# Two transformer stacks on one core: head-pair scores on two row groups, modulation loads and the bias lookup spread over more steps

## The chip, the cores and the metric

The kernel runs on one core of a Trainium2 chip. The metric is the device time in microseconds (us) of one execution. A core has five engines that work side by side, each in the order of its own queue: TensorE (PE, with its weight loads as PEld), VectorE (DVE), ScalarE (ACT), GpSimd (POOL) and SyncE (SP), which here only issues DMAs. TensorE reads weights and moving data from SBUF and writes PSUM, which has eight banks of 128 partitions by 512 fp32 numbers.

## The reference, cut to what matters

`x` has 512 tokens of 1024 features. It goes through a first stack of two layers (latent attention and an MLP, then dilated attention and an MLP) and a second one of two (a recurrent mixer and a gated FFN, a Fourier and convolution mixer and a gated FFN). Every layer is modulated by vectors that are computed from the condition `c`:

```python
cond = silu(c)
mod = (cond @ ada_w[i] + ada_b[i]).reshape(B, N_MOD, D)      # 6 vectors of 1024 for a layer
h = rms_norm(x, norm_mix[i]) * (1 + scale1) + shift1
x = x + gate1 * mixer(h)
h = rms_norm(x, norm_mlp[i]) * (1 + scale2) + shift2
x = x + gate2 * (jnp.square(jax.nn.relu(h @ mlp_w1[i])) @ mlp_w2[i])
```

The dilated mixer has 16 heads of 64 features and three groups (window, dilation) of (128, 1), (512, 4) and (2048, 16). Each group gives scores with a bias that is looked up in a small table, an own softmax, and an output; the three are joined by their softmax denominators:

```python
bias = jnp.moveaxis(bias_table[bucket], -1, 2)
s = jnp.einsum('nbqhd,nbkhd->nbhqk', qb, kb) * (DIL_HEAD_DIM ** -0.5) + bias
lse = jax.nn.logsumexp(jnp.where(valid, s, -jnp.inf), axis=-1)
p = jnp.exp(s - lse[..., None])
o = jnp.einsum('nbhqk,nbkhd->nbqhd', p, vb)
wts = softmax(stack(lses), axis=0)
o = jnp.einsum('gbsh,gbshd->bshd', wts, stack(outs)) @ w_o
```

## The kernel before

`x` is kept transposed, as 8 tiles of 128 features by 512 tokens. All products are fp32 split into a high and a low fp32r part, so that one product is three matmuls (`mm3`: high by high at L423, L427, L428). The stages follow one another: latent attention to about 384 us of the trace, the first MLP (384 to about 810), dilated attention (to about 1495), the second MLP, the recurrent mixer, an FFN (2430 to 2830), the Fourier and convolution mixer, the last FFN.

Weights stream in chunks of 512 KB (`load_w`): SP issues the load into `wst` (two buffers), ACT writes the high part `whi` (L400), DVE the low part `wlo` (L401), three buffers each. One chunk feeds 24 matmuls of 512 columns.

All side work is written as generators, called fibers, in three queues (POST, WORK, LOW). After every six matmuls of a dense product `step()` is called and lets each queue advance by one piece; where a fiber says `yield w` it stands still for w steps. The order on each engine is then made by the framework's scheduler at build time, and each engine keeps it.

Three fibers matter here.

- `ada` computes one modulation vector in two halves. A half loads eight tiles of 256 KB (`adaw`, two buffers, issued by SP at L497, placed behind the latest weight load by `behind`), multiplies each by its condition value and adds it to `adacc` (DVE at L512 and L535, or POOL with two instructions at L532 and L533), splits the sum (`adah` on ACT at L517, `adal` at L518), and then two matmuls of 512 columns (L521, L522) sum over the partitions into the PSUM bank `aux`. The lines that set its steps are

```python
for k in range(KD + 1):
    ...
    yield self.pace
...
yield 4
ps = self.aux.tile([128, T], F32, tag="aux", name="aux")
nc.tensor.matmul(ps, lhsT=self.onesr, rhs=hi, start=True, stop=False)
```

  `pace` is set to 1 before the first MLP and to 2 behind it. In the first MLP, the vectors m105, m111 and m110 are in LOW. The MLP has four parts of 64 steps, 32 for `w1` and 32 for `w2`.
- `dil_bias` looks up the biases in the first MLP: 32 units, 80 chunks, each with two matmuls (L1070) of a one-hot tile `oh` (DVE L1044, made from `ib`, which ACT's queue loads) by the table, an eviction `ev` (L1074 DVE or L1078 ACT) and a store to the DRAM tensors B0 and B12. It yields once for a chunk.
- `attend(pr, x)` is the attention of a pair of heads e=0, 1, whose 64 features each lie in partitions 0 to 63 and 64 to 127 of the same q and k tiles. It runs in WORK beside the next pair's 40 dense steps (`dil_w_in`), for the last pair (7) beside the output product `dil_w_o`, of which the first 768 rows need the pairs 0 to 5 (`os0` to `os5`) and the other 256 the pairs 6 and 7 (`os6`, `os7`). For each head, for w=0 (the dense window) and w=1 (the two dilated groups), SP loads the bias tile `P` (512 KB); then come two sets i=0, 2. A set is one PSUM tile `S` (tag `s`, one buffer): for w=0 six matmuls of 64 rows by 256 columns (two blocks by three of `mm3`), for w=1 four fp32 matmuls of 64 rows by 128 columns (L1199; each is two entries of the trace). DVE adds the bias and takes the maximum (L1210), POOL negates it (L1212), ACT takes exp (L1214). A permutation of the statistics follows on PE (L1222, L1244), POOL scales `P` (L1254), PE turns it (L1267 to L1281) and multiplies by v (L1291 to L1300). PSUM holds `aux` (1 bank), the dense `mm` (2), `s` (1), `t` (2) and `o` (1).

## Time and profile before

| | |
|---|---|
| median of three runs | 3406.11 us (3398.97 to 3411.0) |
| the profiled execution | 3404.87 us |
| its span in the trace | 3403.1 us, so 1.8 us lie outside it |
| PE busy | 3223.0 us, 95% of the span |
| DVE, ACT, POOL busy | 1924.8, 1482.5, 938.7 us |
| TensorE clock granted, mean | 0.976 of full speed |

Busy time is what an engine spends on its instructions; on PE a matmul counts as busy for as long as it runs, at whatever clock. "PEclk" is the granted clock as a share of the full one. Times within a stage are read from windows of the trace; the stages' bounds above come from the same windows.

### The profile page before, as it was taken

To read this page: it belongs to the slowest core of one execution; us is meant where nothing else is said; L and a number is where in the kernel's file an instruction comes from. 1 tells how busy PE (TensorE), PEld (TensorE's weight loads), DVE (VectorE), ACT (ScalarE), POOL (GpSimd) and SP (SyncE) were. 2 spreads that over 40 slices of the span, in tenths; PEclk is the share of its full clock that TensorE was granted. 3 is DMA by queue.
4 is the path that set the end of the run, shared out by engine and by line. 5 is a ranking of instruction groups with operands and counts; after the bars stand their busy time and mean duration, and the time that the engine had idled before them with its cause. 6 is when DMAs were issued, how large, how long until landed. Compare 5 with 4: busy or idle time off the path is not lost.

```text
span 3403.1 us, 46679 instructions
## 1 busy us (share of the span) xinstructions
PE 3223.0 (95%) x17382; PEld 2522.1 (74%) x17382; DVE 1924.8 (57%) x3416; ACT 1482.5 (44%) x2720; POOL 938.7 (28%) x1005
## 2 busy tenths in 40 slices
PE   5898998998999999989999999899899999989998
PEld 4665876887777777768888777667678887778887
DVE  8777655435545434564354577745665556874343
ACT  3565433334555555544242454533342335553232
POOL 5454003002652222103422030350223524540000
PEclk8999999999999999989999999889999999999999
DMA  6433577524344322224544223432144444132222
GB/s 213 129 113 91 168 213 236 168 93 130 118 138 150 128 87 87 78 98 150 156 151 131 69 83 113 105 98 58 66 140 159 162 149 136 56 115 101 95 93 81
DMA packets 234709, 417.40 MB, mean 123 GB/s; under 512 B 66161, under 2 KB 115569, under 8 KB 234481
## 3 DMA queue, kind: packets, MB, share of 16 engines
q1 hardware_dynamic: 217280, 383.82, 35.8%
q10 hardware_dynamic: 17200, 30.58, 3.2%
q8 instruction: 137, 2.24, 0.3%
q14 instruction: 92, 0.75, 0.1%
HBM read 378.64 MB, written 35.69 MB: 122 GB/s over the span
## 4 chain that ended last, share of the span: by engine, by line
PE 76%; DMA 7%; DVE 6%; POOL 4%; ACT 3%; issue 2%; SPq 1%; ACTq 0%; DVEq 0%; POOLq 0%
PE mm L423 20%; PE mm L427 20%; PE mm L428 20%; DMA adaw<-in_ada_w 6%; PE s L1977 1%; POOL adacc L533 1%; DVE nt L676 1%; PE o L2045 1%; DVE h_lo L682 1%; DVE wlo L401 1%; PE s L1199 1%; PE o L954 1%; POOL adaw L532 1%; PE t L938 1%; PE t L2018 1%
## 5 line engine op out<-in xcount | busy, mean ns | idle before, releaser
L427 PE MATMUL mm<-h_lo,whi 128*128 128x512 f32 (+1 forms) x2280 | 889.1, 392 | 17.6 <-DVE h_lo L682 17.6
L423 PE MATMUL mm<-h_hi,whi 128*128 128x512 f32 (+1 forms) x2280 | 875.0, 393 | 18.3 <-ACT whi L400 6.7
L401 DVE TENSOR_TENSOR wlo<-wst,whi 128x1024 fp32r<-128x1024 f32 (+2 forms) x454 | 560.8, 1236 | 577.1 <-ACT whi L400 568.5
L428 PE MATMUL mm<-h_hi,wlo 128*128 128x512 f32 (+1 forms) x2280 | 884.5, 391 | 0.1
L400 ACT ACTIVATE whi<-wst 128x1024 fp32r<-128x1024 f32 (+2 forms) x454 | 455.5, 1005 | 639.1 <-PE mm L427 550.8
L427 PEld LDWEIGHTS mm<-h_lo,whi 128*128 128x128 f32 x2280 | 433.1, 190 | 118.4 <-DVE h_lo L682 24.3
L423 PEld LDWEIGHTS mm<-h_hi,whi 128*128 128x128 f32 x2280 | 427.5, 190 | 120.4 <-ACT h_hi L681 7.9
L428 PEld LDWEIGHTS mm<-h_hi,wlo 128*128 128x128 f32 x2280 | 432.8, 190 | 95.4 <-issue 1.5
L512 POOL TENSOR_SCALAR adacc<-adaw,cond_c 128x512 f32<-128x512 f32 x22 | 20.9, 948 | 788.6 <-DMA adaw<-in_ada_w 537.7
L533 POOL TENSOR_TENSOR adacc<-adacc,adaw 128x512 f32<-128x512 f32 x154 | 216.2, 1404 | 11.7
L427 PE MATMUL mm<-r_lo,whi 128*128 128x512 f32 (+1 forms) x560 | 211.3, 377 | 2.3 <-DVE r_lo L714 2.3
L428 PE MATMUL mm<-r_hi,wlo 128*128 128x512 f32 (+1 forms) x560 | 211.0, 377 | 0.0
L423 PE MATMUL mm<-r_hi,whi 128*128 128x512 f32 (+1 forms) x560 | 210.5, 377 | 0.0
L532 POOL TENSOR_SCALAR adaw<-adaw,cond_c 128x512 f32<-128x512 f32 x154 | 142.7, 927 | 202.2 <-DMA adaw<-in_ada_w 201.1
L535 DVE SCALAR_TENSOR_TENSOR adacc<-adaw,cond_c,adacc 128x512 f32<-128x512 f32 x154 | 121.7, 790 | 90.5 <-DMA adaw<-in_ada_w 89.4
L690 DVE SCALAR_TENSOR_TENSOR x<-mm,m,x 128x512 f32<-128x512 f32 (+1 forms) x130 | 85.4, 690 | 99.0 <-PE mm L428 98.8
L427 PEld LDWEIGHTS mm<-r_lo,whi 128*128 128x128 f32 x560 | 105.5, 188 | 23.8 <-DVE r_lo L714 3.1
L428 PEld LDWEIGHTS mm<-r_hi,wlo 128*128 128x128 f32 x560 | 105.6, 189 | 20.9
L423 PEld LDWEIGHTS mm<-r_hi,whi 128*128 128x128 f32 x560 | 105.6, 189 | 20.9
L1139 POOL TENSOR_TENSOR sq<-raw 128x512 f32<-128x512 f32 x48 | 58.2, 1213 | 156.8 <-ACT raw L1168 37.1
L1214 ACT ACTIVATE P<-P,neg 128x256 f32<-128x256 f32 (+1 forms) x128 | 62.2, 487 | 87.7 <-POOL neg L1212 87.6
L1346 DVE SCALAR_TENSOR_TENSOR u<-mm,vec,u 128x511 f32<-128x511 f32 x44 | 33.0, 749 | 115.9 <-ACT u L1345 115.8
(863 smaller groups left out, 5909.6 us busy)
## 6 DMA issues: line engine op xcount, KB each, us to landing
adaw<-in_ada_w SPq DMA_DIRECT2D x384, 256.0 KB, 3.0
wst<-in_mlp_w SPq DMA_DIRECT2D x128, 512.0 KB, 3.6
wst<-in_ffn_up SPq DMA_DIRECT2D x88, 512.0 KB, 3.6
wst<-in_dil_w_in SPq DMA_DIRECT2D x64, 512.0 KB, 3.5
P<-B SPq DMA_DIRECT2D x32, 512.0 KB, 4.7
wst<-in_ffn_down SPq DMA_DIRECT2D x32, 512.0 KB, 3.4
ib<-ix ACTq DMA_DIRECT2D x64, 129.0 KB, 4.9
B<-msk SPq DMA_DIRECT2D x16, 512.0 KB, 4.7
```

The costliest lines, as they stand in the source:

```text
L400: i = self.nc.scalar.activation(hi, st, AF.Copy)
L401: self.wlo = self.nc.vector.tensor_tensor(lo, st, hi.bitcast(F32), op=ALU.subtract)
L423: i = mm(out, lhsT=l[0], rhs=r[0], start=start, stop=False)
L427: mm(out, lhsT=l[0], rhs=r[1], start=False, stop=False)
L428: mm(out, lhsT=l[1], rhs=r[0], start=False, stop=stop)
L532: eng.tensor_scalar(tmp, a, w, 1.0, op0=ALU.mult, op1=ALU.mult)
L533: eng.tensor_tensor(acc, acc, tmp, op=ALU.add)
L535: eng.scalar_tensor_tensor(acc, a, w, acc, op0=ALU.mult, op1=ALU.add)
L676: nc.vector.scalar_tensor_tensor(t, half_of(self.x[k], h), g[k], r[h], op0=ALU.mult, op1=ALU.mult)
L690: i = self.nc.vector.scalar_tensor_tensor(x, ps, gate[m], x, op0=ALU.mult, op1=ALU.add)
L1139: nc.gpsimd.tensor_tensor(sq, raw, raw, op=ALU.mult)
L1214: nc.scalar.activation(t, t, AF.Exp, bias=neg[:, b:b + 1], accum_out=total[:, b:b + 1])
```

## The change

There are four edits. In `ada` the wait between the split and the two matmuls is six steps and not four. `pace` becomes 2 in `mlp`, as soon as the first `w1` product of a part has been written, instead of behind the whole first MLP: m105, which is then past its loads, is not touched, but m111 and m110 go at one load in two steps. `dil_bias` yields two steps a chunk. And `attend` is turned: the loop over w is outermost, then i; the score matmuls of both heads of a set are issued alternately, head 0 on partitions 0 to 63 and head 1 on 64 to 127, into two `S` tiles. For that `s` has two buffers, so that all eight banks are taken. There is a `yield` between matmuls and softmax, so that the count of steps stays 8. The two bias tiles of a w are loaded together.

```diff
@@ ada
             eng.tensor_tensor(lo, a, hi.bitcast(F32), op=ALU.subtract)
-            yield 4
+            yield 6
             ps = self.aux.tile([128, T], F32, tag="aux", name="aux")
@@ mlp
                 self.dense(f"mlp_w1_{l}", D, n, h, sink, psum, first=half_of if part == 0 else None)
+                self.pace = 2
                 self.dense(f"mlp_w2_{l}", n, D, r, self.residual(gate, end), psum, last=half_of if end else None)
@@ dil_bias
                     ib = load(*units[i + 2])
-                yield
+                yield 2
             done = (gi, q0, ev)
@@ dilated
-            sp = E(tc.tile_pool(name="dil_s", bufs=1, space=PSUM))
+            sp = E(tc.tile_pool(name="dil_s", bufs=2, space=PSUM))
@@ attend
-                for e in range(2):
-                    hd = pr * 2 + e
-                    o = slice(e * 64, e * 64 + 64)
-                    for w in range(2):
+                rows = [slice(e * 64, e * 64 + 64) for e in range(2)]
+                for w in range(2):
+                    mx, total = {}, {}
+                    for e in range(2):
+                        hd = pr * 2 + e
                         p = P[e, w] = work.tile([128, 4, 256], F32, tag="P", name="P", bufs=5)
...
+                    for i in (0, 2):
+
+                        S = [sp.tile([128, 2, 256], F32, tag="s", name="s") for e in range(2)]
+                        units = [[], []]
+                        for j in range(2):
+                            b = i + j
+                            if w:
+                                for g in range(2):
+                                    for e, o in enumerate(rows):
+                                        mm(S[e][:, j, g * 128:g * 128 + 128], lhsT=res(x[f"q{1 + g}"][o], b),
                                            rhs=res(x[f"k{1 + g}"][o], b), start=True, stop=True)
...
+                            else:
+                                k0 = min(max(128 * b - 64, 0), 256)
+                                for n, (a, c) in enumerate(((0, 0), (0, 1), (1, 0))):
+                                    for e, o in enumerate(rows):
+                                        mm(S[e][:, j], lhsT=res(x["q0"][a][o], b), rhs=x["k0"][c][o][:, k0:k0 + 256],
+                                           start=n == 0, stop=n == 2)
...
+                        yield
+                        for e in range(2):
...
+                        yield
@@ build
             n.mlp(0, g, sh, "m105", MLP_PARTS[0], 5)
-            n.pace = 2
```

**Modulation loads in the first MLP.** On SP's queue before, around the second half of m110 (`adaw` are its loads, `wst` the weight chunks; a weight load waits there for a free `wst` buffer):

```order
L497 DMA adaw_5018<-in_ada_w 128x512
L497 DMA adaw_5037<-in_ada_w 128x512
L390 DMA wst_5362<-in_mlp_w2_0 128x1024
L497 DMA adaw_5079<-in_ada_w 128x512
L497 DMA adaw_5098<-in_ada_w 128x512
L390 DMA wst_5408<-in_mlp_w2_0 128x1024
L497 DMA adaw_5116<-in_ada_w 128x512
L390 DMA wst_5440<-in_mlp_w2_0 128x1024
```

The eighth load of the half is adaw_5116. On PE before, the matmul that needs all eight (L521) stands among the matmuls of the chunk that was loaded as wst_5330, the one ahead of wst_5362:

```order
L423 MATMUL mm_5336<-h_hi5_3542,whi_5332 128x512
L427 MATMUL mm_5336<-h_lo5_3543,whi_5332 128x512
L521 MATMUL aux_5243<-adah_5157,onesr_82 128x512
L428 MATMUL mm_5336<-h_hi5_3542,wlo_5333 128x512
L423 MATMUL mm_5337<-h_hi5_3542,whi_5332 128x512
```

So the last load stands behind the second weight load after the chunk in which PE reaches L521, 16 of the 24 matmuls short of that chunk's end. On SP's queue after, the end of a half of m110 (its first one):

```order
L497 DMA adaw_4986<-in_ada_w 128x512
L390 DMA wst_5079<-in_mlp_w2_0 128x1024
L497 DMA adaw_5011<-in_ada_w 128x512
L497 DMA adaw_5037<-in_ada_w 128x512
L390 DMA wst_5128<-in_mlp_w2_0 128x1024
L390 DMA wst_5187<-in_mlp_w2_0 128x1024
```

and on PE after, the L521 of that half, behind the last matmul of the chunk wst_5079 (`whi_5081`):

```order
L427 MATMUL mm_5086<-r_lo7_5076,whi_5081 128x512
L428 MATMUL mm_5086<-r_hi7_5075,wlo_5082 128x512
L521 MATMUL aux_5175<-adah_5108,onesr_82 128x512
L522 MATMUL aux_5175<-adal_5109,onesr_82 128x512
L423 MATMUL mm_5193<-r_hi0_4704,whi_5130 128x512
```

Now the last load stands behind the weight load of the very chunk at whose end L521 stands. Counted in chunks, the place of L521 minus that of the last load (0 where L521 stands at the start of the chunk whose weight load is just ahead of that load) is -1.6, -1.9, -1.3 and -1.6 for the four halves of m111 and m110 before, and +0.8, +0.8, +1.0 and 0.0 after; ten halves in the second MLP, before, have -0.9 to +1.3.

**Scores.** On PE before, one set of w=0 of one head among the dense matmuls of the next pair:

```order
L423 MATMUL mm_7745<-h_hi0_6915,whi_7641 128x512
L423 MATMUL s_7654<-k0h_7196,q0h_7358 128x256
L427 MATMUL s_7654<-k0l_7197,q0h_7358 128x256
L428 MATMUL s_7654<-k0h_7196,q0l_7359 128x256
L427 MATMUL mm_7745<-h_lo0_6916,whi_7641 128x512
```

Of the six matmuls three are shown; the three of the next block read alike. After, two sets stand together, and the heads change at every matmul (s_8281 is head 0, s_8282 head 1):

```order
L428 MATMUL mm_8085<-h_hi7_6929,wlo_8081 128x512
L1210 MATMUL s_8281<-k0h_7813,q0h_8066 128x256
L1210 MATMUL s_8282<-k0h_7813,q0h_8066 128x256
L1210 MATMUL s_8281<-k0l_7814,q0h_8066 128x256
L1210 MATMUL s_8282<-k0l_7814,q0h_8066 128x256
L1210 MATMUL s_8281<-k0h_7813,q0l_8067 128x256
L1210 MATMUL s_8282<-k0h_7813,q0l_8067 128x256
```

Over all w=0 sets, 169 of the 176 possible changes of head are there. Of the w=1 sets, those of i=0 alternate as written; those of i=2 mostly stand like this, on PE after:

```order
L1202 MATMUL s_8413<-k1_7925,q1_8123 128x128
L1202 MATMUL s_8413<-k2_8013,q2_8170 128x128
L1202 MATMUL s_8413<-k1_7925,q1_8123 128x128
L1202 MATMUL s_8413<-k2_8013,q2_8170 128x128
L1202 MATMUL s_8414<-k1_7925,q1_8123 128x128
L1202 MATMUL s_8414<-k2_8013,q2_8170 128x128
```

Four matmuls of one head come ahead of four of the other (two of the latter are shown); 61 of 112 possible changes are there. All 64 sets of before stand in 40 groups now, 16 for w=0 and 24 for w=1.

**The last pair beside the output product.** On PE before, from the first permutation of pair 7 (L1222) on:

```order
L428 MATMUL mm_12725<-os6h_12711,wlo_12694 128x512
L1222 MATMUL s_12461<-w4_12459,dil_perm_7013 128x64
L423 MATMUL mm_12726<-os6h_12711,whi_12693 128x512
L427 MATMUL mm_12726<-os6l_12712,whi_12693 128x512
L428 MATMUL mm_12726<-os6h_12711,wlo_12694 128x512
L1244 MATMUL s_12494<-w4_12459,dil_perm_7013 128x32
L1267 MATMUL t_12538<-ident_84,P_12334 128x128 x4
L1267 MATMUL t_12545<-ident_84,P_12424 128x128 x2
```

Behind L1244 no dense matmul follows until `os7h` is there. After, from the second permutation on (L1254 there, the turns are L1277):

```order
L427 MATMUL mm_12562<-os4l_12300,whi_12557 128x512
L1254 MATMUL s_12526<-w4_12491,dil_perm_7013 128x32
L1277 MATMUL t_12570<-ident_84,P_12409 128x128
L428 MATMUL mm_12562<-os4h_12299,wlo_12558 128x512
L1277 MATMUL t_12570<-ident_84,P_12409 128x128
L423 MATMUL mm_12562<-os5h_12303,whi_12557 128x512
L1277 MATMUL t_12570<-ident_84,P_12409 128x128
L427 MATMUL mm_12562<-os5l_12304,whi_12557 128x512
```

Pair 7 now stands earlier in the output product: 46 dense matmuls lie between its second permutation and the first one that reads `os7h`, where there were none.

## Rows read from the trace of the kernel before

**Rows 1.** Page, part 1: busy us, share, instructions.

```profile
PE 3223.0 (95%) x17382; PEld 2522.1 (74%) x17382; DVE 1924.8 (57%) x3416; ACT 1482.5 (44%) x2720; POOL 938.7 (28%) x1005
```

**Rows 2.** Windows: stretch, us, busy PE PEld DVE ACT POOL, PEclk, DMA share, GB/s.

```profile
480.00:500.00 20.00, 15.16 (x62) 11.78 (x62) 11.83 (x23) 4.66 (x9) 0.00 (x0) 0.91 0.71 189
520.00:540.00 20.00, 15.85 (x64) 12.42 (x63) 7.92 (x16) 7.80 (x15) 6.01 (x7) 0.91 0.71 188
560.00:580.00 20.00, 15.20 (x59) 11.90 (x58) 12.72 (x22) 6.38 (x11) 6.83 (x6) 0.91 0.63 201
640.00:800.00 160.00, 160.00 (x694) 129.03 (x693) 58.43 (x63) 57.76 (x83) 1.08 (x1) 1.00 0.30 100
840.00:1454.00 614.00, 608.96 (x3095) 467.68 (x3093) 292.14 (x657) 335.76 (x685) 205.55 (x270) 1.00 0.35 113
```

**Rows 3.** PE's waits in the first MLP: us in total, times, longest.

```profile
PE aux L521 <- ACT adah L517: 13.8, 3, 4.8
PE look L1070 <- ACT ev L1078: 2.9, 3, 1.9
...
PE aux L521 <- ACT ssq L655: 1.7, 1, 1.7
```

**Rows 4.** Timeline of PE behind one such wait: start, us.

```profile
493.17 0.63 PE L427 MATMUL mm<-r_lo,whi 128*128 128x512 f32 x1
493.60 0.63 PE L428 MATMUL mm<-r_hi,wlo 128*128 128x512 f32 x1
```

**Rows 5.** DVE's waits in that stage, then POOL's timeline.

```profile
DVE adacc L535 <- DMA adaw<-in_ada_w: 25.3, 15, 4.1
...
525.60 0.70 POOL L532 TENSOR_SCALAR adaw<-adaw,cond_c 128x512 f32<-128x512 f32 x1 [5.32 <-DMA adaw<-in_ada_w]
```

**Rows 6.** Timeline of PE: a score set of w=0, one of w=1.

```profile
981.74 0.40 PE L423 MATMUL mm<-h_hi,whi 128*128 128x512 f32 x1
...
982.28 0.28 PE L427 MATMUL s<-k0l,q0h 64*128 64x256 f32 x1
982.40 0.28 PE L428 MATMUL s<-k0h,q0l 64*128 64x256 f32 x1
...
982.97 0.50 PE L427 MATMUL mm<-h_lo,whi 128*128 128x512 f32 x1
983.31 0.40 PE L428 MATMUL mm<-h_hi,wlo 128*128 128x512 f32 x1
...
967.39 1.16 PE L1199 MATMUL s<-k,q 64*128 64x128 f32 x8
968.48 0.50 PE L428 MATMUL mm<-h_hi,wlo 128*128 128x512 f32 x1
```

**Rows 7.** Timeline of PE in the recurrent mixer: halves of 64 rows alternating.

```profile
1928.42 0.49 PE L1830 MATMUL hU<-hv,kt 64*128 64x128 f32 x4
```

**Rows 8.** Windows (as rows 2) and PE's timeline at dilated attention's end.

```profile
1454.00:1476.00 22.00, 17.15 (x93) 10.19 (x92) 3.60 (x14) 6.72 (x15) 7.10 (x16) 0.76 0.08 25
1476.00:1484.00 8.00, 7.61 (x20) 5.57 (x21) 5.14 (x6) 3.30 (x5) 0.00 (x0) 0.58 0.37 123
...
1457.19 0.38 PE L1244 MATMUL s<-w,dil_perm 128*128 128x32 f32 x2 [1.84 <-DVE w L1240]
...
1475.22 0.73 PE L423 MATMUL mm<-os7h,whi 128*128 128x512 f32 x2 [1.36 <-ACT os7h L367]
```

**Rows 9.** Page, part 6 (bias tiles), then instructions of L1210 (ns min/median/max).

```profile
P<-B SPq DMA_DIRECT2D x32, 512.0 KB, 4.7
...
L1210 DVE CUSTOM_DVE_ANT_1 P<-s,P x64: 408/420/448, 890.8 to 1452.7; 128x256 f32<-128x256 f32 x64
```

**Rows 10.** Page, part 5, POOL; then PE's wait from 2830 us on.

```profile
L533 POOL TENSOR_TENSOR adacc<-adacc,adaw 128x512 f32<-128x512 f32 x154 | 216.2, 1404 | 11.7
...
L532 POOL TENSOR_SCALAR adaw<-adaw,cond_c 128x512 f32<-128x512 f32 x154 | 142.7, 927 | 202.2 <-DMA adaw<-in_ada_w 201.1
...
PE mm L423 <- ACT y4h L367: 7.2, 1, 7.2
```

More of the change, by code (lines that the diff above doesn't have):

```diff
@@ L1189, in attend @@
                             nc.sync.dma_start(out=p, in_=self.B0[:, hd].rearrange("b p j -> p b j"))
-                        mx, total = (st[:, 1, j, e] if w else nt[:, j, e] for j in range(2))
-                        neg = sm.tile([128, 4], F32, tag="neg", name="neg", bufs=4)
-                        for i in (0, 2):
-                            S = sp.tile([128, 2, 256], F32, tag="s", name="s")
-                            units = []
-                            for j in range(2):
-                                b = i + j
-                                if w:
-                                    for g in range(2):
-                                        mm(S[:, j, g * 128:g * 128 + 128], lhsT=res(x[f"q{1 + g}"][o], b),
-                                           rhs=res(x[f"k{1 + g}"][o], b), start=True, stop=True)
-                                    units.append((b, S[:, j].rearrange("p (g j) -> p g j", g=2), by_res[e][:, b]))
-                                else:
-                                    k0 = min(max(128 * b - 64, 0), 256)
-                                    self.mm3(S[:, j], [res(t[o], b) for t in x["q0"]], [t[o][:, k0:k0 + 256] for t in x["k0"]],
-                                             True, True)
-                                    c0, c1 = band(b)
-                                    s0 = 128 * b - 64 + c0 - k0
-                                    units.append((b, S[:, j, s0:s0 + c1 - c0], p[:, b, c0:c1]))
-                            for b, s, t in units:
-                                nc.vector.tensor_tensor_reduce(out=t, in0=s, in1=t, scale=1.0, scalar=-3e38,
-                                                               op0=ALU.add, op1=ALU.max, accum_out=mx[:, b:b + 1])
-                            nc.gpsimd.tensor_scalar(neg[:, i:i + 2], mx[:, i:i + 2], -1.0, 0.0, op0=ALU.mult, op1=ALU.add)
-                            for b, s, t in units:
-                                nc.scalar.activation(t, t, AF.Exp, bias=neg[:, b:b + 1], accum_out=total[:, b:b + 1])
-                            yield
@@ new lines, in attend @@
+                        mx[e], total[e] = (st[:, 1, j, e] if w else nt[:, j, e] for j in range(2))
+                    for i in (0, 2):
[7 more added lines that the diff above has]
+                                        mm(S[e][:, j, g * 128:g * 128 + 128], lhsT=res(x[f"q{1 + g}"][o], b),
+                                           rhs=res(x[f"k{1 + g}"][o], b), start=True, stop=True)
+                                for e in range(2):
+                                    units[e].append((b, S[e][:, j].rearrange("p (g j) -> p g j", g=2), by_res[e][:, b]))
+                            else:
[4 more added lines that the diff above has]
+                                           start=n == 0, stop=n == 2)
+                                c0, c1 = band(b)
+                                s0 = 128 * b - 64 + c0 - k0
+                                for e in range(2):
+                                    units[e].append((b, S[e][:, j, s0:s0 + c1 - c0], P[e, w][:, b, c0:c1]))
+                        yield
+                        for e in range(2):
+                            neg = sm.tile([128, 4], F32, tag="neg", name="neg", bufs=4)
+                            for b, s, t in units[e]:
+                                nc.vector.tensor_tensor_reduce(out=t, in0=s, in1=t, scale=1.0, scalar=-3e38,
+                                                               op0=ALU.add, op1=ALU.max, accum_out=mx[e][:, b:b + 1])
+                            nc.gpsimd.tensor_scalar(neg[:, i:i + 2], mx[e][:, i:i + 2], -1.0, 0.0, op0=ALU.mult, op1=ALU.add)
+                            for b, s, t in units[e]:
+                                nc.scalar.activation(t, t, AF.Exp, bias=neg[:, b:b + 1], accum_out=total[e][:, b:b + 1])
+                        yield
```

## The prediction

> **What bounds the kernel now.** I began with the page's busy times: PE is busy in 95% of the span and the next engine in 57% [rows 1], so time can only be won where PE idles, runs slower than it could, or does work that can be shortened. Windows of 20 to 600 us then show which stage has what. A stretch of pure dense work in the first MLP is full: 160.00 of 160 us busy with 694 matmuls at clock 1.00, which gives 160/694 = 0.2305 us for a dense matmul of 512 columns [rows 2]. So is nearly all of dilated attention, 608.96 of 614 us [rows 2]: what is cut from PE's work there comes off the time, as long as the other engines keep up; they are busy for a third to a half of it.
>
> Three stretches are not full or not short. First, the first MLP from 480 to 580 us, where three windows have 15.16, 15.85 and 15.20 busy us of 20 and a clock of 0.91 [rows 2]. PE's list of waits names the cause: the matmul of a modulation vector (L521) waits for the split of its sum three times, 13.8 us in all [rows 3]. Behind each wait matmuls start 0.43 us apart for a while (493.17, 493.60) [rows 4], nearly twice 0.2305: PE idled, and then ran at the lower of its two clock levels. What the sum waits for is the transfer: DVE stands 25.3 us in 15 waits for the tiles `adaw`, and POOL, which sums m110, waits 5.32 us for a tile whose last product PE needs 5 us later [rows 5]. Second, the score matmuls, which use only half of the array's rows. Third, the end of dilated attention: from 1454 to 1476 us PE is busy for 17.15 of 22 us at clock 0.76, and then for 7.61 of 8 us at 0.58 [rows 8].
>
> **A, modulation loads and lookups in the first MLP.** No instruction is added or removed; sixteen loads each of m111 and m110, their sums, the matmuls L521 and the lookups move to later steps. In the order before, L521 stands 1.3 to 1.9 chunks ahead of where its last load stands on SP's queue, after it stands 0.0 to 1.0 chunks behind. A chunk is 24 x 0.2305 = 5.5 us, so each half gets about two chunks, 11 us, and a wait was 4.8 us at most [rows 3]. The second MLP is the check: its ten halves have -0.9 to +1.3, and PE's waits there list none at L521. I take all three waits as gone: 13.8 us. The slow clock behind them goes too: 1.00 - 0.91 = 0.09 of 20 us is 1.8 us for each of three windows, 5.4 us [rows 2]. Of the waits for lookups, 2.9 us [rows 3], I count a third, since the one-hot tiles get more time but the chunks on PE are only some 12% further apart by the order. L521's wait for the norm's statistics, 1.7 us [rows 3], I leave in: in the order after, a vector's matmul stands at the norm again. The transfers that move go to a stretch with DMA share 0.30 instead of 0.71 [rows 2], where PE does not wait for weights. A = 13.8 + 5.4 + 1.0 = 20 us. Below, 7 us, if two of the three waits come back at their old length, 20 - 2 x (4.6 + 1.8); above, 26 us, if all lookup and norm waits go and some small ones beside them.
>
> **B, scores on two row groups.** Before there are 8 pairs x 2 heads x 2 sets = 32 sets of each kind. A w=0 set: from the dense matmul at 981.74 to the one at 983.31 there are 1.57 us, of which two dense matmuls (981.74 and 982.97) take 0.46, so the set costs 1.11 us [rows 6]. Its matmuls start 0.12 us apart (982.28, 982.40) [rows 6], six of them 0.72, so that 0.39 us is entering and leaving. A w=1 set takes 1.09 us from its first entry to the next dense matmul (967.39 to 968.48) [rows 6]; with the same 0.2 us of delay at the dense matmuls around it, it costs 1.29, of which eight slots of 0.112 are 0.90 and 0.39 again the edges. In all 32 x 1.11 + 32 x 1.29 = 77 us of PE.
>
> Does a pair on both halves overlap? No score matmul shows it, but L1830 does: four matmuls of 64 rows that alternate between the halves end 0.49 us after their start [rows 7], where four of L1199, all in one half, would take 1.16 - 4 x 0.112 = 0.71 (durations of rows 6 and 7). The difference, 0.22 us, is two slots for two pairs. So I count one slot saved for each change of head that the second matmul of a pair makes. For w=0, which alternates throughout, twelve matmuls take six slots: 16 groups x 6 x 0.12 = 11.5 us saved, and 16 edges of 0.39 fewer, 6.2 us. For w=1, 61 changes of head stand in the order after, since an entry's second pass follows in the same half and the sets of i=2 mostly go four and four: 61 x 0.112 = 6.8 us; 24 groups instead of 32 save 8 x 0.39 = 3.1 us. B = 11.5 + 6.2 + 6.8 + 3.1 = 28 us. Below: nothing overlaps and only the edges are saved, 9 us. Above: all w=1 sets overlap wholly, 112 instead of 61 slots and 8 more edges saved, 28 + 5.7 + 3.1 = 36 us.
>
> The Trainium skill's page "TensorEngine Tiling (Array Packing)", Overview, Theoretical Speedup, gives up to a factor of two where the contraction is 64 or less, and names no order in which the matmuls must stand. By it every slot of w=1 would be halved as well, which is the upper end just given; the one row that bears on it (L1830) alternates at every matmul, so no row shows what four and four do.
>
> What must keep up: the softmax of a set (L1210, two instructions of 0.42 us for a head, four for both) [rows 9] now comes at once for both heads, 1.7 us of DVE ahead of the low parts of the weights (L401) that are queued behind it. Those are one chunk, 5.5 us, ahead of PE, so I count nothing; without this cover it would cost up to 1.7 us for each of 32 groups, 54 us. The two loads of `P` are 512 KB each and land after 4.7 us (median) [rows 9]; that is the rival below.
>
> **C, the end of dilated attention.** Of the 22 us, 4.85 are idle; at 0.76 the 17.15 busy us lose 4.1; in the next 8 us, 0.4 idle and 0.42 x 7.61 = 3.2 are lost: 12.5 us [rows 8]. The reason is in the order: between pair 7's second permutation (1457.19) and the first matmul of `os7h` (1475.22) [rows 8] PE has only the turning and multiplying of pair 7, which wait for POOL's scaling and ACT's copies in turn. After, 46 dense matmuls, 10.6 us, stand in between, and the scores of that pair come earlier in the output product too. They cover the scaling, but not all: the last turns stand close to `os7h` again. C = 10 us; 0 if the dense matmuls wait for the same things in order, 12.5 if nothing is left.
>
> **D, losses elsewhere.** `pace` 2 holds from the first MLP on either way, but the two more steps a half stretch the vectors of the FFN: six vectors (m2012 and five behind it) now need 6 x 2 x (18 + 6) = 288 steps, before 264, and the FFN has 264. So a half of m2110 runs on into the next mixer: three of its products on POOL and the split stand there in the order after, ahead of the convolution's taps. A product is 0.93 + 1.40 us [rows 10]; with a split of 1.3 us, as POOL's L533 runs, three are 8.3 us. PE has one wait of 7.2 us there, at `y4h`, behind that convolution [rows 10], and it could grow by them all; POOL has room before its first tap, so I count 2 (0 to 8).
>
> Sum: 20 + 28 + 10 - 2 = 56 us. The profiled execution takes 3404.87 us, 1.8 of them outside its span and unchanged; 3404.87 - 56 = 3349 us. The median shown is 1.2 us above that execution, which is less than the runs differ.
>
> **Rivals.**
>
> *The row groups do not overlap* (the edit does not do what it says): B is 9 instead of 28, 3368 us. For it: PE takes its instructions in order, and each fp32 entry reloads its weights. Against: L1830 [rows 7].
>
> *Full overlap:* the four matmuls of one head start before the four of the other are through, since they share neither rows nor bank; B is 36, 3341 us. Against: in the rows a matmul starts behind the one ahead of it in the order [rows 6], and half the w=1 sets go four and four. The page named above would have this case.
>
> *The first MLP's waits stay:* the loads are spread, but they still stand behind weight loads that wait for their buffers, so the last of a half comes late; A is 7, 3362 us. For it: the last half has a lead of 0.0 chunks only. Against: the second MLP at the same leads.
>
> *The tail is not covered:* C is 0, 3359 us.
>
> *Slower:* a set's two `P` loads land one after the other, L1210 of the first head holds DVE in order, the low weight parts queue up behind it, and PE runs dry. There are 16 such pairs of loads; each that held PE for one landing, 4.7 us [rows 9], would cost 75 us in all, 3424 us. It decides from 56/16 = 3.5 us for each pair on. For it: DVE's order is fixed, and the second tile is wanted sooner after its issue than before. Against: L401 works a chunk, 5.5 us, ahead, so a hold must be longer than that before PE sees it, and the DMA share is 0.35 there [rows 2].
>
> **How the numbers follow.** Forecast 0.65, rivals in the order above 0.12, 0.06, 0.08, 0.05 and 0.04. The range: downward full overlap with A at 26 and D at 0 gives 3349 - 8 - 6 - 2 = 3333, with C at its end 3330, and I put 3328; upward the row groups' failure together with returned waits gives 3349 + 19 + 13 = 3381, and 3384 with some of D. The likeliest case alone has 3335 to 3368. Under 0.3%, 10 us, this kernel's measurement cannot tell a change. All cases but the last lie over 10 us below 3406; a mild form of the last would make it no change: faster 0.92, same 0.04, slower 0.04.
>
> **What would show it.** A right: no wait at L521 for `adah` in the first MLP, clock 1.00 in every window from 480 to 580. B right: a w=0 group of twelve within 1.2 us of PE, w=1 groups of i=0 shorter than those of i=2, and dilated attention from 840 to its tail shorter by some 25 to 30 us. C right: idle time and low clock around `os7h` down to 2 or 3 us. D: the wait at `y4h` longer than 7.2 us by 2. Wrong would be: twelve w=0 matmuls in 1.8 us, waits of PE for `wlo` in dilated attention with DVE at L1210 ahead of them, or new waits at L521 in the FFN or the second MLP.

## The result and the profile after

The changed kernel takes 3368.86 us, median of four runs (3362.55 to 3370.5), against 3404.61 us for the kernel before (four runs, 3398.97 to 3411.0): the ratio is 0.9891 (95% interval 0.9869 to 0.9913). That is 36 us where 56 were forecast; it lies in the range. Its profiled execution took 3370.5 us. The page of the profile after, its span and the line that answers to [rows 1]:

```profile
span 3368.7 us, 46642 instructions
...
PE 3191.8 (95%) x17382; PEld 2504.8 (74%) x17382; DVE 1923.2 (57%) x3416; ACT 1478.4 (44%) x2720; POOL 932.9 (28%) x1005
```

PE's share is unchanged at 95%, on a span that is 34.4 us shorter. Where they went is read by stage. Every stage begins with a norm whose first matmul sums the squares (L654), so the distance from one such start to the next in PE's timeline is the length of a stage:

| stage | before, us | after, us | difference | forecast |
|---|---|---|---|---|
| first MLP | 425.1 | 406.7 | -18.4 | A -20 |
| dilated attention with `dil_w_o` | 686.4 | 661.0 | -25.4 | B -28 and C -10 |
| second MLP | 370.0 | 372.0 | +2.0 | 0 |
| recurrent mixer | 582.0 | 582.7 | +0.7 | 0 |
| first gated FFN | 387.9 | 387.5 | -0.4 | 0 |
| Fourier and convolution mixer | 173.4 | 180.3 | +6.9 | D +2 |
| last FFN, to the last norm | 381.0 | 381.0 | 0.0 | 0 |

**First MLP.** Windows of that stage of the kernel after (columns as in [rows 2]):

```profile
480.00:500.00 20.00, 20.00 (x91) 15.99 (x91) 11.26 (x17) 4.99 (x9) 0.00 (x0) 1.00 0.83 235
520.00:540.00 20.00, 20.00 (x91) 16.03 (x90) 7.96 (x7) 8.25 (x15) 13.41 (x12) 1.00 0.71 203
540.00:560.00 20.00, 16.81 (x68) 13.21 (x68) 9.10 (x13) 8.38 (x15) 5.72 (x5) 0.91 0.57 163
560.00:580.00 20.00, 20.00 (x88) 16.13 (x87) 13.57 (x25) 3.24 (x4) 8.00 (x7) 1.00 1.01 314
640.00:790.00 150.00, 150.00 (x689) 122.80 (x688) 60.37 (x68) 51.34 (x71) 8.19 (x7) 1.00 0.32 115
```

Where 480, 520 and 560 read 0.91 before, they read 1.00 and are full. New holes have come at 540 us and, smaller, at 580 us (17.89 busy us of 20); from 640 us to the stage's end PE is full, as before. PE's waits in that stage of the kernel after name their cause:

```profile
PE look L1071 <- ACT ev L1079: 5.2, 4, 3.2
PE look L1071 <- DVE ev L1075: 2.1, 1, 2.1
```

None is at L521 any more (13.8 us in [rows 3]). The lookups wait instead, 7.3 us where they had 2.9.

**Scores.** PE's timeline of the kernel after: a w=0 group, a w=1 group of i=0, a w=1 group of i=2, each with the dense matmul behind it:

```profile
1173.72 0.39 PE L1210 MATMUL s<-k0h,q0h 64*128 64x256 f32 x2
1173.94 0.28 PE L1210 MATMUL s<-k0l,q0h 64*128 64x256 f32 x2
1174.06 0.28 PE L1210 MATMUL s<-k0h,q0l 64*128 64x256 f32 x2
...
1174.62 0.50 PE L423 MATMUL mm<-h_hi,whi 128*128 128x512 f32 x1
...
1180.15 1.16 PE L1202 MATMUL s<-k,q 64*128 64x128 f32 x16
1181.24 0.50 PE L423 MATMUL mm<-h_hi,whi 128*128 128x512 f32 x1
...
1185.64 1.71 PE L1202 MATMUL s<-k,q 64*128 64x128 f32 x16
1187.28 0.50 PE L423 MATMUL mm<-h_hi,whi 128*128 128x512 f32 x1
```

Two w=0 matmuls (x2) start in each slot, 0.12 us apart; the group of twelve takes 1174.62 - 1173.72 = 0.90 us, as long as six took before [rows 6]. The alternating w=1 group of sixteen entries takes 1181.24 - 1180.15 = 1.09 us, as eight took before. The one that goes four and four takes 1.64 us. The 40 groups of the order after are 23 of w=0 and 17 of w=1, in the trace and in the kernel's order alike, not 16 and 24; before, the 64 sets stood in 40 and 34 pieces, since dense matmuls cut some of them.

**What took half of that back.** Windows of dilated attention after:

```profile
840.00:900.00 60.00, 54.93 (x268) 42.98 (x267) 31.37 (x81) 32.52 (x71) 38.05 (x40) 0.96 0.41 136
900.00:960.00 60.00, 60.00 (x327) 45.49 (x326) 23.74 (x53) 28.48 (x56) 34.37 (x40) 0.95 0.41 131
960.00:1020.00 60.00, 55.38 (x278) 42.15 (x279) 31.45 (x65) 35.62 (x74) 25.18 (x32) 0.94 0.41 133
1020.00:1080.00 60.00, 56.05 (x299) 43.02 (x298) 31.45 (x71) 32.14 (x66) 20.81 (x28) 0.94 0.34 106
1140.00:1200.00 60.00, 60.00 (x328) 46.19 (x326) 31.90 (x79) 36.42 (x79) 14.10 (x20) 1.00 0.35 118
```

Before, the stretch from 840 to 1454 us has clock 1.00 and 5 us of idle time in 614 [rows 2]. After, its first 240 us have 13.6 us of idle time. The clock takes 0.04, 0.05, 0.06 and 0.06 of the busy time there, 11.9 us at most: the mean clock of a window also covers time in which PE stood still, and counted matmul by matmul (each start to the next, half of it where the clock stood at the lower level) it is 10.3 us. From 1140 us to the tail the stage is full again. PE's waits in those 240 us of the kernel after, and ACT's wait for the negation there, before (L1214) and after:

```profile
PE mm L423 <- ACT raw L1167: 7.2, 3, 4.6
PE t L1277 <- POOL P L1264: 5.0, 6, 1.2
...
ACT P L1214 <- POOL neg L1212: 32.9, 19, 5.1
ACT P L1224 <- POOL neg L1222: 34.4, 11, 7.9
```

`raw` is the eviction of a dense tile; PE waited 2.1 us for it there before. The turns of `P` (L1277) wait for POOL's scaling. In total ACT waits for the negation no longer than before, but in 11 pieces instead of 19, and in longer ones. The longest hole, followed through four engines of the kernel after (DVE, POOL, ACT, PE; in brackets the idle time and its releaser):

```profile
955.50 0.08 DVE L1220 DVE_READ_ACCUMULATOR2_ANT st<- 128x1 f32 x1
...
959.30 0.69 POOL L532 TENSOR_SCALAR adaw<-adaw,cond_c 128x512 f32<-128x512 f32 x1 [1.22 <-DMA adaw<-in_ada_w]
960.08 1.26 POOL L533 TENSOR_TENSOR adacc<-adacc,adaw 128x512 f32<-128x512 f32 x1
961.32 0.19 POOL L1222 TENSOR_SCALAR neg<-st 128x2 f32<-128x2 f32 x1
...
961.54 0.51 ACT L1224 ACTIVATE P<-P,neg 128x256 f32<-128x256 f32 x1 [7.90 <-POOL neg L1222]
...
963.52 1.05 ACT L1167 ACTIVATE raw<-mm 128x512 f32<-128x512 f32 x1
...
964.62 0.79 PE L423 MATMUL mm<-h_hi,whi 128*128 128x512 f32 x1 [4.62 <-ACT raw L1167]
965.21 0.63 PE L427 MATMUL mm<-h_lo,whi 128*128 128x512 f32 x1
965.64 0.63 PE L428 MATMUL mm<-h_hi,wlo 128*128 128x512 f32 x1
```

DVE has both maxima of the first head at 955.58. POOL waits for a modulation tile, multiplies and adds it, and only then, at 961.32, 5.7 us later, comes to the negation of these maxima, which takes 0.19 us. ACT has stood still for 7.90 us, does the exps of both heads, and at 963.52 reaches `raw`, which is queued behind them. PE needs that bank: 4.62 us idle, and then, with starts 0.6 and 0.43 us apart, the lower of its two clock levels, where it had run at 1.00.

**The end of dilated attention.** Windows around the first matmul of `os7h` after, and that matmul:

```profile
1418.00:1434.00 16.00, 14.61 (x104) 9.87 (x102) 4.25 (x6) 6.19 (x11) 0.00 (x0) 1.00 0.16 50
1434.00:1442.00 8.00, 6.13 (x24) 4.35 (x24) 7.88 (x10) 4.76 (x7) 0.00 (x0) 1.00 0.43 146
...
1432.04 0.73 PE L423 MATMUL mm<-os7h,whi 128*128 128x512 f32 x2 [1.36 <-ACT os7h L367]
```

The clock stays at 1.00, and the idle time is 1.4 and 1.9 us, where [rows 8] had 4.85 and 0.4 and the clock at 0.76 and 0.58. The wait at `os7h` itself is the same 1.36 us.

**The mixer behind the FFN.** POOL's timeline after, where the convolution's taps (L1402, L1392 before) begin:

```profile
2830.18 2.33 POOL L532 TENSOR_SCALAR adaw<-adaw,cond_c 128x512 f32<-128x512 f32 x2 [9.96 <-DMA adaw<-in_ada_w]
...
2833.73 1.29 POOL L1402 TENSOR_TENSOR cp<-cp,tap 128x512 f32<-128x512 f32 x1
2834.99 2.28 POOL L533 TENSOR_TENSOR adacc<-adacc,adaw 128x512 f32<-128x512 f32 x1
2837.22 1.29 POOL L1402 TENSOR_TENSOR cp<-cp,tap 128x512 f32<-128x512 f32 x1
```

POOL first waits 9.96 us for a modulation tile, so the first tap starts 40.2 us into the stage instead of 36.1. Two sums, a product and the split of m2110 then stand between the first five taps; a tap by itself costs 1.3 us. PE's wait at `y4h` is 7.2 us as in [rows 10]; the stage is 6.9 us longer because what leads up to it comes later.

### The profile page after: what moved, and what is told of

The parts are those of the page before. It is cut to its first block, busy times and chain, and to the rows that moved or that the text cites. A ratio compares the mean times of both kernels' runs of the same rounds, so it can differ in the third digit from the quotient of the medians.

```text
span 3368.7 us, 46642 instructions
## 1 busy us (share of the span) xinstructions
PE 3191.8 (95%) x17382; PEld 2504.8 (74%) x17382; DVE 1923.2 (57%) x3416; ACT 1478.4 (44%) x2720; POOL 932.9 (28%) x1005
## 4 chain that ended last, share of the span: by engine, by line
PE 78%; DVE 8%; DMA 4%; POOL 4%; ACT 3%; issue 2%; SPq 0%; ACTq 0%; DVEq 0%; POOLq 0%
PE mm L423 21%; PE mm L427 20%; PE mm L428 20%; DMA adaw<-in_ada_w 4%; DVE nt L676 1%; PE s L1987 1%; POOL adacc L533 1%; DVE h_lo L682 1%; POOL cp L1402 1%; POOL adaw L532 1%; PE o L2055 1%; DVE wlo L401 1%; PE look L1071 1%; PE t L2028 1%; PE o L955 1%
## 5 line engine op out<-in xcount | busy, mean ns | idle before, releaser
L517 ACT ACTIVATE adah<-adacc 128x512 fp32r<-128x512 f32 x44 | 27.7, 629 | 147.6 <-POOL adacc L533 105.3
```

## Experiments

Each kernel ran beside the kernel before, whose median was 3407.06 us with the first four, 3412.41 with the next four and 3409.5 with the last four. Times of single executions of one kernel differ by 5 to 15 us, so what an edit does is read from the stage in its trace as well; the stage lengths are those of the table's kind. They vary too: with dilated attention as in the kernel after, the six traces of after, e2, e4, e5, e8 and e12 have 657.3 to 661.0 us for it, and the eleven traces with the pacing of the kernel after in the first MLP, or with four steps in place of six, have 406.4 to 415.5 us there.

**One half of the change at a time.** `e1` has only the three pacing edits, `e2` only the attend with its two S buffers.

```diff
 # e1, against the kernel before
-            yield 4
+            yield 6
...
+                self.pace = 2
...
-                yield
+                yield 2
...
-            n.pace = 2
```

> Kernel before with the three pacing edits alone (six steps, pace 2 in the MLP, two steps a lookup chunk). If the parts add up as the trace after splits them (first MLP 18.7 us shorter, the start of the Fourier and convolution mixer 6.6 us longer): 3404.6 - 12 = 3392.5 us, no wait at L521 in the first MLP. Rival, the pacing edits are worth nothing by themselves or hurt dilated attention too: 3400 or more.

Measured: 3395.86 us, ratio 0.9969 (0.9959 to 0.9979). First MLP 406.5 us (-18.6), dilated attention 688.9, Fourier and convolution mixer 180.0 (+6.6). The parts of the trace hold.

```diff
 # e2, against the kernel after
-            yield 6
+            yield 4
...
-                self.pace = 2
...
-                yield 2
+                yield
...
+            n.pace = 2
```

> Kernel before with the turned attend and two S buffers alone. Theory (the new waits of the first head pairs come from the turned attend itself, whose negations and exps come in bursts): dilated attention 6 us shorter in its body and 17 in its tail, 3404.6 - 23 = 3381 us, clock below 1.00 in several windows of the first 240 us of dilated attention. Rival (those waits come from the modulation vectors that the six steps moved): the body gains the whole 30 us, 3357 us, clock 1.00 there.

Measured: 3383.27 us, ratio 0.9931 (0.9917 to 0.9944). Dilated attention 659.9 us (-26.4, 23 expected), the first MLP 425.8 and the mixer 172.5 as before. The product of the two ratios is 0.990, the change's is 0.9891: the halves add up. PE's waits at L521 for `adah` in the first MLP of e2 are there again, 11.9 us in three, and the windows of its dilated attention have losses of the same kind:

```profile
840.00:900.00 60.00, 57.91 (x273) 45.62 (x272) 28.40 (x59) 30.39 (x60) 26.57 (x27) 0.97 0.46 142
900.00:960.00 60.00, 56.30 (x292) 42.53 (x291) 29.49 (x55) 32.79 (x62) 36.65 (x44) 0.94 0.43 135
960.00:1020.00 60.00, 56.52 (x282) 44.51 (x281) 34.45 (x84) 34.33 (x75) 35.48 (x43) 0.94 0.45 143
1020.00:1080.00 60.00, 58.74 (x320) 45.16 (x319) 31.15 (x83) 33.45 (x72) 17.01 (x27) 1.00 0.40 121
```

That is 10.5 us of idle time, where the kernel before has 2.7. The single waits are others: 2.7 us for `raw`, 3.7 for DVE's `w`, 2.7 at L521 and L522. So new waits come with the turned attend, not with the loads that were moved, and which ones come depends on what else stands in the queues. The rival, 3357 us, is out.

**The negation on another engine.** `e3` moves the negation of the maxima from POOL to DVE.

```diff
-                            nc.gpsimd.tensor_scalar(neg[:, i:i + 2], mx[e][:, i:i + 2], -1.0, 0.0, op0=ALU.mult, op1=ALU.add)
+                            nc.vector.tensor_scalar(neg[:, i:i + 2], mx[e][:, i:i + 2], -1.0, 0.0, op0=ALU.mult, op1=ALU.add)
```

> Kernel after with the negation of the maxima on VectorE instead of GpSimd. Theory (a negation of 0.19 us stands on GpSimd behind the products of a modulation vector that wait for their loads; ACT's exps wait for it in order, the eviction of a dense tile behind them, and PE for that): ACT's wait for the negation falls from 34 us to under 10 between 840 and 1080 us, PE's waits for raw from 8.1 to under 4, clock 1.00 in most windows there; 12 to 17 us gained, 3354 us. Rival (the eight exps of two heads in one piece, 5 us of ACT, hold the eviction back whoever negates): 3366 to 3370 us, waits for raw as before.

Measured: 3370.99 us, ratio 0.9897 (0.9881 to 0.9912), no gain. ACT's waits of that kernel from 840 to 1080 us:

```profile
ACT P L1224 <- DVE neg L1222: 18.0, 7, 6.6
```

It fell from 34.4 to 18.0 us, not under 10. The hole near 960 us is gone, PE's waits for `raw` are 5.9 us (8.1 after), two windows have 0.97 and the rest 1.00, and dilated attention took 654.4 us in that execution. In `e10`, with the same negation, it took 658.3; the kernels with it on POOL have 657.3 to 661.0. The negation's place is thus worth a few us at most, not 12 to 17, and e10's 658.3 leaves open whether it is worth anything: the theory names the longest hole rightly and is not the whole cause. The rival's time, 3366 to 3370 us, is nearly met, its waits for `raw` are not.

**The modulation sums away from POOL.** `e9` leaves the negation on POOL and takes what it stood behind away.

```diff
-                                            nc.gpsimd if l and j % 2 == 0 else nc.vector))
+                                            nc.gpsimd if l and j == 0 else nc.vector))
```

> Kernel after with the sums of m112 and m114, the two modulation vectors that GpSimd computes beside the first head pairs, on VectorE. Theory (the products that wait for their loads hold the negation on GpSimd): ACT's wait for the negation between 840 and 1080 us falls from 34 to under 15 us, the wait of 4.6 us for raw near 960 us goes, dilated attention 6 to 10 us shorter than in the two traces of the kernel after (748.6 and 746.2 us from its first dense matmul to the output product's end). Rival (the exps of two heads hold the eviction, or VectorE's sums now hold the additions of the bias in the same way): 743 us or more, and raw waits of 7 us or more.

PE's wait for `raw` in dilated attention of that kernel:

```profile
PE mm L423 <- ACT raw L1167: 5.3, 4, 1.5
```

Dilated attention took 649.0 us in this one trace, 8 to 12 less than in those of the kernel after (6 to 10 were expected). From 840 to 1080 us PE is idle for 6.1 us, 13.6 after: it waits 3.9 us for `raw`, the longest 1.5, and 2.2 for the scaling of `P`. ACT's wait for the negation fell only to 23.8 us. The median of the five runs is 3372.82 us; one of them took 3408.74, the others 3358.24 to 3374.19, and the ratio without it is 0.9877 (0.9855 to 0.9898). The control e5 has 0.9881, so the time does not show the gain: in this trace the recurrent mixer, which the edit does not touch, took 593.1 us at a mean clock of 0.94, where the kernel after has 582.7 at 0.96.

**The steps between split and matmul.** `e4` goes back to four everywhere, `e8` only from the recurrent mixer on.

```diff
 # e4
-            yield 6
+            yield 4
 # e8
-            yield 6
+            yield self.rest
...
-        self.pace = 2
+        self.pace, self.rest = 2, 6
...
+        n.rest = 4
         for l, (name, f) in enumerate((("ab", n.ab), ("cd", n.cd))):
```

> Kernel after with four steps instead of six between split and matmul; the rest of the pacing stays. Theory (six steps make the FFN's vectors 288 steps long where it has 264, and the rest of m2110 delays the taps on GpSimd): 6.6 us come back at the start of the Fourier and convolution mixer, 3362 us, with the first MLP still without waits at L521, since its leads only fall by half a chunk. Rival (the two steps are what removed the waits of the first MLP): up to 13 us of waits come back there, 3375 us.

> Kernel after with four steps between split and matmul from the recurrent mixer on, six before it. Theory (the FFN's six vectors fit its 264 steps again, and GpSimd reaches the taps without products of m2110 among them): the Fourier and convolution mixer begins and ends 6.6 us earlier, 3362 us. Rival (the taps are late for another reason, VectorE's and ACT's order): 3369 us.

Measured: e4 3369.57 us (ratio 0.9889, 0.9874 to 0.9905), e8 3364.87 us (0.9865, 0.9849 to 0.9881), against 3370.95 for the kernel after beside it (e5). In e4 the mixer is back to 175.6 us and the first MLP unchanged at 406.4, without the rival's waits; that gain of 4.7 us does not show in the median. In e8 the mixer takes 173.0 us, 7.3 less than after and as before, and the median is 6.1 lower. POOL's timeline of e8 has the last split of m2110 ahead of the taps, which stand together, 1.6 us each:

```profile
2800.34 1.27 POOL L518 TENSOR_TENSOR adal<-adacc,adah 128x512 fp32r<-128x512 f32 x1 [0.74 <-ACT adah L517]
...
2833.09 17.65 POOL L1402 TENSOR_TENSOR cp<-cp,tap 128x512 f32<-128x512 f32 x11 [31.11 <-ACT tap L1401]
```

**The changed kernel once more.** `e5` is the kernel after, as control.

> The changed kernel once more, as the control for the three that run with it. If the waits in the first head pairs belong to the order of the queues: the same places (the first w=1 sets of pairs 0 to 2) with raw waits of 5 to 9 us in all and three or four stretches of low clock between 840 and 1080 us, 3367 to 3372 us. If they are an accident of one execution: clock 1.00 there and a time 15 us lower.

Measured: 3370.95 us, ratio 0.9881 (0.9864 to 0.9897). PE's waits for `raw` 8.9 us in five, the longest 4.7 at 960.68 us, and low clock in four stretches from 895 to 1056 us. The holes belong to the order of the queues. Dilated attention 657.3 us, first MLP 408.6.

**The order of the heads.** `e6` holds all matmuls of head 0 in a set ahead of those of head 1, `e7` makes them alternate everywhere; both collect the matmuls of a set in a list and chain them with order edges, e6 after sorting by head.

```diff
+                        todo.sort(key=lambda t: t[0])
+                        prev = None
+                        for _, out, l, r, first, end in todo:
+                            m = mm(out, lhsT=l, rhs=r, start=first, stop=end)
+                            if prev is not None:
+                                self.order(prev, m)
+                            prev = m
```

(e7 is without the first of these lines.)

> Kernel after, but within each set all matmuls of head 0 come ahead of those of head 1, held by order edges. Theory (two row groups run side by side only where the heads change): w=0 groups of twelve take 1.6 us or more instead of 0.91, all w=1 groups of eight 1.64 instead of 1.09; PE loses 16 x 0.7 + 8 x 0.55 = 16 us, 3384 us. Rival (what is saved is only the entering and leaving of a group): groups as long as in the kernel after, 3369 us.

Measured: 3384.69 us, ratio 0.9914 (0.9898 to 0.9929), 13.7 us over the control; in its trace 8.7 of them lie in dilated attention (666.0 us). PE's timeline of a w=0 group of e6:

```profile
1177.14 0.38 PE L1219 MATMUL s<-k0h,q0h 64*128 64x256 f32 x1
...
1177.48 0.28 PE L1219 MATMUL s<-k0h,q0l 64*128 64x256 f32 x1
1177.49 0.39 PE L1219 MATMUL s<-k0h,q0h 64*128 64x256 f32 x2
1177.71 0.28 PE L1219 MATMUL s<-k0l,q0h 64*128 64x256 f32 x2
1177.83 0.28 PE L1219 MATMUL s<-k0h,q0l 64*128 64x256 f32 x2
1177.95 0.28 PE L1219 MATMUL s<-k0h,q0h 64*128 64x256 f32 x1
...
1178.39 0.50 PE L423 MATMUL mm<-h_hi,whi 128*128 128x512 f32 x1
```

From 1177.14 to 1178.39 are 1.25 us, between the 0.90 of the alternating group and the 1.6 expected. Three slots hold two matmuls: the row at 1177.49 is head 1's first, which starts beside head 0's third (1177.48), and head 0's fourth, which starts at 1177.60; 1177.71 and 1177.83 are one of each head (by the single starts and the longer first record of a head). So head 1's first matmul runs ahead of three of head 0's that stand before it in the order. The w=1 groups are 1.64 us, as expected, but for those that a wait follows and two at the stage's end. The length of a group follows the order of the heads, and the rival is out.

> Kernel after with order edges that make the heads alternate in every set, the w=1 sets of i=2 too. Theory (alternation is all that those sets lack): their groups fall from 1.64 to 1.09 us, 8 x 0.55 = 4 us, 3365 us. Rival (the first head's matmuls now wait for the second head's S buffer, so what is won in the array is lost in front of it): 3369 us or more, with a wait at L1202 for st.

Measured: 3375.67 us, ratio 0.9891 (0.9873 to 0.9909), single runs from 3369.13 to 3381.67, against 0.9881 of the control: no gain. All w=1 groups that no wait follows are 1.09 us. Summed over the stage from the starts in the trace (each start to the next, idle time taken out, low clock counted half), score matmuls took 65.6 us before, 39.3 after, 33.8 in e7; but the dense matmuls with the output product, 465.7 after, and the products with v (`o`), 36.6 after, took 469.8 and 40.8 in e7. Why these grew is not settled. Dilated attention is 657.1 us, the control 657.3. The first MLP, which the edit does not touch, took 415.5 us in this trace and 408.6 in the control's, so the higher time says nothing about the order of the heads.

**The lookups' pace.** `e12` is the kernel after with one step a lookup chunk.

```diff
-                yield 2
+                yield
```

> Kernel after with one step a lookup chunk again; the loads' pace and the six steps stay. Theory (the waits at L521 went with the loads' pace, the lookups add nothing): the first MLP within 3 us of the kernel after (337.8 and 338.5 us from the 600th to the 1900th dense matmul, 354.3 before). Rival (the lookups' transfers compete with the modulation loads, and their half pace is needed): 345 us or more, with waits at L521.

Measured: 3385.2 us, ratio 0.9927 (0.9913 to 0.9941). First MLP 421.4 us. PE's waits there in e12:

```profile
PE look L1071 <- DVE ev L1075: 5.1, 2, 4.3
PE look L1071 <- ACT ev L1079: 4.5, 5, 2.3
PE mm L423 <- ACT r_hi L713: 3.9, 1, 3.9
```

Neither side is right in full: the stage is back at 421.4 us, as the rival has it, but there is no wait at L521. The waits have moved to the lookups, 9.6 us, and to the relu's split, 3.9. The lookups' half pace without the loads' was not run.

**Versions that join the gains.** `e10` is e8 with the negation on DVE, `e11` has the forced alternation as well.

> Kernel after with the late four steps of e8 and the negation on VectorE of e3. If both gains are real and add up: 6 us from the taps and 6 from dilated attention, ratio to the kernel before 0.985, some 3359 us where the kernel after has 3371. If the negation is worth nothing in the time: as e8, 0.9865.

> As e10, and the forced alternation of e7. Score matmuls 33.8 us of PE as in e7 instead of 39.3. If what they save comes off the time once the negation is out of GpSimd's queue: 4 us under e10. If it only turns up in the dense and output matmuls around the groups, as in e7: the same as e10.

Measured: e10 3367.86 us, ratio 0.988 (0.9866 to 0.9894); e11 3361.07 us, ratio 0.9864 (0.9847 to 0.988), single runs from 3354.66 to 3364.47. Both have the mixer at 174.7 and 175.0 us. Their dilated attention is 658.3 and 655.9 us. e10 gains nothing over e8. e11's time is the lowest of all, but its ratio is e8's, 0.9865, and of the difference to e10 only 2.4 us lie in dilated attention, while the recurrent mixer took 593.8 us in e10's trace and 579.4 in e11's. What can be said to gain over the changed kernel is e8's edit, by its stage; in the time its interval, 0.9849 to 0.9881, still overlaps with the control's, 0.9864 to 0.9897, and so does e11's.

## Why the prediction held, and where its steps did not

The direction and the range were right, the size was 20 us too large (56 forecast, 36 measured). The time alone would have misled: 3368.86 us lies just outside the 3335 to 3368 that the prediction gives to its likeliest case, and on the 3368 of the rival without overlap. That it lies in the range is in part luck: the range was stretched for that rival, and what cost the time was something else. Only the stages show that. By the table 12.6 us are missing in dilated attention, 4.9 in the mixer, 2.0 in the second MLP and 1.6 in the first; the second MLP's 2.0 is no more than that stage varies (370.0 to 374.0 us in all traces).

**A, 20 us: 18.4 measured**, by the right mechanism with a wrong split. The waits at L521 and the lower clock behind them went, as the leads of the order said. The size is less sure than it looks, since the traces with this pacing have 406.4 to 415.5 us, 10 to 19 less than before. But the step "Of the waits for lookups, 2.9 us [rows 3], I count a third", 1 us, was mis-sized: without the lookups' half pace only 3.7 of the 18.4 us are left (e12, 421.4 us, above all those traces), since PE then waits for the lookups' evictions instead. The loads' pace removes one wait, the lookups' pace keeps the next one from taking its place. What it leaves is the 7.3 us above.

**B, 28 us net: about 16 measured** (25.4 of the stage less C). The saving itself was larger than forecast. All PE work of the stage, each start to the next without idle time and with low clock counted half, fell from 652.8 to 616.0 us; score matmuls are 65.6 - 39.3 = 26.3 us of it. Of these some 6 are the leaving of groups (0.90 - 6 x 0.12 = 0.18 us for each of 34 that went) and 20 are slots, where the sum has 11.5 + 6.8 = 18.3. "One slot saved for each change of head" was too low for w=1. An alternating set saves eight of sixteen slots (1.09 us, as half as many entries took before), and one change of head in the middle saves three (e6). The edges were too low as well: 74 pieces became 40, so 34 went and not 24. The speedup of up to two that the Trainium skill gives ("TensorEngine Tiling (Array Packing)", Overview, Theoretical Speedup) is reached in this trace by the sets that alternate, 0.90 and 1.09 us, and not by those that go four and four, 1.64 us.

The step that failed is the cover: "What must keep up ... so I count nothing". It weighed DVE alone, whose additions are short, and left out the two engines behind it. The exps of both heads now stand together on ACT, in order ahead of the evictions `raw`, and they wait for negations on POOL, in order behind modulation sums that wait for DMAs. With two `mm` banks PE has little slack. The 5.0 us in which PE's turns wait for POOL's scaling of `P` fall to 2.2 in e9 and 1.8 in e3; what makes that scaling late is not settled. From 840 to 1080 us that is 13.6 us of idle time and 10.3 of low clock where the kernel before has about 3 and none. Shown: that new waits come with the turned attend (e2), that they recur (e5), that the longest hole goes with the negation's place (e3), and that with the sums of m112 and m114 off POOL the stage is 8 to 12 us shorter (e9, one trace). Argued only: that the bunching of the negations, and not their total, which is as before, is what PE feels; and that the rest, waits for `raw` of 1 to 2 us which e3 and e9 keep, is ACT's run of exps itself. No run spread the exps.

**C, 10 us: 9 measured.** In [rows 8] 12.5 us are lost; after, 1.39 + 1.87 = 3.3 us. The loss did not move behind: from there to the next norm PE is idle for 5.7 us before and 6.2 after. The 46 dense matmuls that now stand ahead of `os7h` cover the scaling; no run takes them out alone.

**D, 2 us: 6.9 measured.** The mechanism was right (e8 removes it), the size was not: "POOL has room before its first tap" is refuted by POOL's timeline: the first tap starts 4.1 us late in the stage, behind a wait for a load, and two sums, a product and the split hold up the next ones. The bound of 8.3 us was the better estimate.

**The rivals.** Row groups that do not overlap: refuted by the groups and by e6. Full overlap: right where heads alternate. Waits that stay in the first MLP: not at L521. A tail without cover: no. The slower one, loads of `P` in pairs that hold DVE until PE runs dry of low weight parts: PE's waits of that stage after have none for `wlo`; the stall came, but through ACT and POOL.

## What to carry to other kernels

Where work is cut on the engine that binds, ask of every engine in the loop, not only of the next one, what now comes in one piece and who is queued behind it in order; a 0.19 us instruction behind a waiting one cost 4.6 us here and the lower clock after it. When a wait is removed by spreading loads, look which wait is next in the same stage, and spread that too: the loads alone gave 3.7 us (e12), both gave 18. For matmuls of 64 rows, pair the halves matmul by matmul.

## What the runs showed of the hardware

Matmuls on the two halves of the array overlap even when they are not interleaved: in e6 three pairs ran together around one change of head. The holes of up to 4.6 us on PE between 840 and 1080 us, 13.6 us in all, cost three quarters as much again through the lower clock level behind them (10.3 us). And the recurrent mixer, which no edit touches, took from 578.5 to 593.8 us in the traces, at mean clocks of 0.94 to 0.96; differences of a few us elsewhere can only be read by stage, and there against what the stage varies by itself.
